# Gate/up projection by 2x2 block algebra: two weight sums made by accumulating DMAs, 18 of 22 tiles by it in place of 14

## The chip, the cores and the metric

The kernel runs on one core of a Trainium2 chip. The metric is the device time of one execution in microseconds. The kernel before took 859.75 us (median of 3 runs, 854.94 to 861.74).

## The reference

One layer of a hybrid decoder for 512 tokens of width 1024, in float32: an RMS norm, an input projection, two causal mixers (HGRN2 and gated DeltaNet), their gated merge, an output projection and a residual, and then a SwiGLU feed-forward block. The change lies in the feed-forward block:

```python
v = rms_norm(h, pre_ffn_w)
gate, up = jnp.split(jnp.einsum('btd,df->btf', v, w_gate_up), 2, axis=-1)
f = jnp.einsum('btf,fd->btd', jax.nn.silu(gate) * up, w_down)
return h + rms_norm(f, post_ffn_w)
```

Here v is 512 x 1024, w_gate_up is 1024 x 5632 (2816 gate and 2816 up columns) and w_down is 2816 x 1024.

## The kernel before, in words

**Numbers.** Each float32 operand of a product is split in two: `hi`, a rounded copy made on ScalarE (ACT), and `lo`, the rest, made by a subtraction on VectorE (DVE). A product is then three matmuls on TensorE (PE): hi x hi, hi x lo, lo x hi (L116 to L118, or L1010 to L1012).

**Stages.** Input projection and mixers, merge, `out_proj` (from about 430 to 490 us), `ffn` (gate and up products and SiLU, L1022, to 713 us) and `down` (L1102, to the end). The feed-forward width 2816 is cut in 22 tiles of 128 columns, `ft` 0 to 21 in the loop of L1076. A tile has a gate weight block g and an up weight block u, each 128 partitions x 1024 values: the first 512 are the rows of w_gate_up that belong to the first half of v's width, the other 512 those of the second half.

**Direct tiles** (before: ft 0, 1, 4, 7, 10, 13, 16, 19). `wload` (L99) loads g and then u into a `raw` buffer (512 KB each, two buffers of that tag), splits it into `whi` and `wlo` (three buffers of each), and 8 x 3 matmuls of 512 columns follow for each. Then ACT and DVE work out silu(gate) * up.

**Tiles by block algebra** (the others; `winograd`, L959, Winograd's variant of Strassen). The 2x2 matrix of weights is B11 = first half of g, B12 = first half of u, B21 and B22 = second halves of g and u. The 2x2 matrix of activations is v cut in token halves and width halves; its sums S1 to S4 are made once by `block_sums` (L924). Seven products of half the width and half the tokens replace eight: 7 x 4 x 3 matmuls of 256 columns. Four sums of weight blocks are needed in every tile. They are made on DVE: `t13`, one instruction over 1024 values that makes two of them, and `t24`, two instructions of 512 values. `t13` and `t24` lie in the two `raw` buffers. Seven operands (three blocks and four sums) are split by `operand` (L913), two to one `whi`/`wlo` buffer. The blocks themselves come by four SP DMAs of 256 KB into `raw = slot(5 + ft % 2)`, so two tiles have such a slot. The products accumulate in three PSUM tiles X, Wb and Y; DVE combines them with five instructions (`s15`, `s16`, `c22`, `c12`, `c21`), ACT copies `s1`. Product 6, `c21` and the SiLU of a tile (`flush`, L1062) come after products 0 and 1 of the next tile.

**Order.** A scheduler that works at build time puts the instructions of each engine in an order by priority, and allots buffers in turn by tag; at run time each engine and each DMA queue takes its instructions strictly in that order and waits on semaphores. `winograd` makes its weight sums and splits under a raised priority, loads have a higher one. In `ffn` the SP queue issues all weight loads; the POOL (GpSimd) engine has no work in the tile loop and no instruction after 489 us.

Of the kernel before, what the change touches and what calls it, by code (L numbers as in the profile page):

```python
# [9 lines left out]
F32 = mybir.dt.float32  # L10
# [4 lines left out]
ALU = mybir.AluOpType  # L15

P = 128
# [6 lines left out]
NF = DFF // P  # L24
EPS = 1e-6
NEG = -30000.0
HG_LEVELS = (64, 32, 16, 8, 4, 2, 1)
HG_MASKS = (16, 8, 4, 2, 1)

# [14 lines left out]
class K:  # L44
# [570 lines left out]
    def hg_attn(self, c, out):  # L615
# [20 lines left out]
        yield  # L636
        for lev in HG_LEVELS[:-1]:
            v = lambda x: x.rearrange("p h (n two t) -> p (h n) two t", two=2, t=lev)
# [194 lines left out]
    def out_proj(self):  # L833
# [4 lines left out]
        for nh in range(2):  # L838
            for lst, tile_, nm in ((pmw, self.hct, "post_mix_w"), (pfw, self.st, "pre_ffn_w")):
                t = tile_()  # L840
                lst.append(t.rearrange("p h t -> p (h t)"))
                nc.gpsimd.dma_start(out=lst[nh], in_=self.I[nm][nh * 512:nh * 512 + 512].partition_broadcast(P))
        W = []
        for i in range(8):
# [9 lines left out]
            for j in range(2):  # L854
                raw = self.dct((P, 512))
                nc.sync.dma_start(out=raw, in_=self.I["w_out"][i, :, j * 512:j * 512 + 512])
                self.split(h_[:, j, :], l_[:, j, :], raw, nc.gpsimd if i % 2 else None)
            W.append((h_, l_))
        self.h = []
# [64 lines left out]
    def block_sums(self, A, tmp, dst):  # L924


        hi, lo = A
        H, L = slice(256, 512), slice(0, 256)
        g = self.nc.gpsimd
        out = dict(A11=(0, L), A12=(1, L), A22=(1, H))  # L930
        out = {n: [[x[i][:, k, t] for k in range(4)] for x in A] for n, (i, t) in out.items()}
        S_ = [([], []) for _ in range(4)]
        for j in (slice(0, 2), slice(2, 4)):
            def block(i, t, eng=None):
                a = tmp()
                self.tt(a, hi[i][:, j, t].bitcast(F32), lo[i][:, j, t].bitcast(F32), ALU.add, eng)
                return a

            def put(i, src):
                d = dst(i, j)  # L940
                self.split(d[0], d[1], src)
                for o, x in zip(S_[i], d):
                    o += [x[:, 0], x[:, 1]]

            a21, a22 = block(0, H), block(1, H)
            self.tt(a22, a21, a22, ALU.add)
            put(0, a22)
            a11 = block(0, L, g)
            self.tt(a21, a11, a21, ALU.subtract)
            put(2, a21)  # L950
            self.tt(a22, a22, a11, ALU.subtract)
            put(1, a22)
            a12 = block(1, L, g)
            self.tt(a12, a12, a22, ALU.subtract)
            put(3, a12)
        out.update({f"S{i + 1}": S_[i] for i in range(4)})
        return out

    def winograd(self, raw, A, c12, c21, c22):  # L959

        nc = self.nc
        with self.tc.high_priority(offset=200):
            B11, _, B22, B21 = (raw[:, i] for i in range(4))
            t13, t24 = (self.wp.tile([P, 1040], F32, tag="raw", name=self.name("raw"), bufs=2)[:, :1024]
                        .rearrange("p (i n) -> p i n", i=2) for _ in range(2))
            self.tt(t13, raw[:, 1:3], raw[:, 0:2], ALU.subtract)
            self.tt(t24[:, 0], B22, t13[:, 0], ALU.subtract)
            self.tt(t24[:, 1], B21, t24[:, 0], ALU.subtract)  # L970
            W = [[t.rearrange("p (k f) -> p k f", k=4) for t in self.operand(x)]
                 for x in (B11, t13[:, 0], t24[:, 0], B21, t13[:, 1], B22, t24[:, 1])]
        X, Wb, Y = (f((P, 256)) for f in (self.mm_ps, self.dps, self.hps))
        prod = lambda i, a, ps, start: self.product(i, W[i], A[a], ps, start)
        s1, s15, s16 = (self.ftmp() for _ in range(3))
        now = self.tc.high_priority

        def first():
            prod(0, "A11", X, True)
            with now():  # L980
                nc.scalar.copy(s1, X)
            prod(1, "S1", Wb, True)
            with now():
                self.tt(s15, Wb, s1, ALU.add)

        def second():
            prod(2, "S2", Y, True)
            with now():
                self.tt(s16, Y, s1, ALU.add)
            prod(3, "A12", X, False)  # L990
            prod(4, "S3", Y, False)
            with now():
                self.tt(c22, Y, s15, ALU.add)
            prod(5, "S4", Wb, False)
            with now():
                self.tt(c12, Wb, s16, ALU.add)

        def third():
            prod(6, "A22", Y, False)
            with now():  # L1000
                self.tt(c21, Y, s1, ALU.add)

        return X, first, second, third

    def product(self, i, W, A, ps, start):
        wh, wl = W
        ah, al = A
# [14 lines left out]
    def ffn(self):  # L1022

        nc = self.nc
        A = nc.scalar
        self.half = self.fhalf = None
        gt = []

        def gslot(i):
            if i % 4 == 0:  # L1030
                gt.append(self.slot((4, 13, 11, 12, 14, 15)[i // 4], [P, 4, S]))
            return gt[i // 4][:, i % 4, :]

        def mms(ps, w, ts):
            for k in range(KD):
                self.mm3(ps[:, ts], w[0][:, k, :], w[1][:, k, :], self.vhi[k // 4][:, k % 4, ts],
                         self.vlo[k // 4][:, k % 4, ts], k == 0, k == KD - 1)

        load = lambda ft, gu: self.wload(self.I["w_gu"][ft, gu], (P, KD, P))

        def evac(t, g, u):
            with self.tc.high_priority():
                self.sigmoid(t, g)
                self.tt(t, t, g, ALU.mult)
                self.tt(t, t, u, ALU.mult)

        bank = lambda gu: self.hps((P, 512)) if gu else self.mm_ps()

        first = [(0, 0), (0, 1), (1, 0)]
        ws = {p: load(*p) for p in first}  # L1050
        pss = {p: bank(p[1]) for p in first}
        for half in range(2):
            for p in first:
                mms(pss[p], ws[p], slice(half * 256, half * 256 + 256))
        sp = [self.slot(i, [P, 4, 2, 256]) for i in (14, 15)]
        sp = iter([t[:, i] for t in sp for i in range(4)])
        so = [self.slot(i, [P, 2, 4, 256], F32R) for i in range(4)]
        L = self.block_sums((self.vhi, self.vlo), lambda: next(sp), lambda i, j: (so[i][:, 0, j], so[i][:, 1, j]))
        lo, hi = slice(0, 256), slice(256, 512)
        pending = None  # L1060

        def flush():  # L1062
            nonlocal pending
            if pending:
                X, third, g, u, t = pending
                third()
                A.activation(t[:, lo], X, AF.Exp, scale=-1.0)
                A.activation(t[:, hi], g[:, hi], AF.Exp, scale=-1.0)
                A.activation(t, t, AF.Ln, bias=self.one)
                A.activation(t, t, AF.Exp, scale=-1.0)  # L1070
                self.tt(t[:, lo], t[:, lo], X, ALU.mult)
                self.tt(t[:, hi], t[:, hi], g[:, hi], ALU.mult)
                self.tt(t, t, u, ALU.mult)
            pending = None

        for ft in range(NF):  # L1076
            if ft < 2 or ft % 3 == 1:
                for gu in range(2):
                    if (ft, gu) not in ws:
                        pss[ft, gu] = bank(gu)  # L1080
                        mms(pss[ft, gu], load(ft, gu), slice(0, S))
                    if gu == 0:
                        flush()
                evac(gslot(ft), pss[ft, 0], pss[ft, 1])
                continue
            with self.tc.high_priority():
                raw = self.slot(5 + ft % 2, [P, 4, 512])

                for gu in range(2):
                    src = self.I["w_gu"][ft, gu].rearrange("p (a b) -> p a b", a=2)  # L1090
                    nc.sync.dma_start(out=raw[:, gu], in_=src[:, 0])
                    nc.sync.dma_start(out=raw[:, 3 - gu], in_=src[:, 1])
            g, u = self.hct((P, 512)), self.hct((P, 512))
            X, p1, p2, p3 = self.winograd(raw, L, u[:, lo], g[:, hi], u[:, hi])
            p1()
            flush()
            p2()
            pending = X, p3, g, u, gslot(ft)
        flush()
        self.gt = gt  # L1100
# [116 lines left out]
def layouts(i):  # L1217
# [28 lines left out]
    t = np.arange(P)  # L1246
    cm = [np.eye(P), t[:, None] <= t[None, :], np.where(t[:, None] <= t[None, :], 0.0, NEG)]
    blk = lambda h: ((t[:, None] // (2 * h) == t[None, :] // (2 * h))
# [22 lines left out]
```

## Time and profile before

| | |
|---|---|
| median of 3 runs | 859.75 us (854.94 to 861.74) |
| the profiled execution | 856.85 us, span 855.1 us |
| PE busy | 823.5 us (96%) |
| DVE busy | 581.2 us (68%) |
| ACT busy | 487.2 us (57%) |
| POOL busy | 137.4 us (16%) |
| DMA | 96.43 MB, mean 113 GB/s |
| granted clock of PE | 0.984 of full speed over the span, 1.00 from 400 to 800 us |

A busy time is the time in which an engine executes at least one instruction, and the durations of neighbouring instructions overlap: what an engine needs for one is the distance between the starts of two that follow each other without a wait. The matmuls above all are pipelined. A group of instructions is written as line, engine, operation, out<-in with the program's tile names, and shape; tiles that come from `slot` appear as `s`.

### The profile page before, as it was taken

To read this page: it belongs to the slowest core of one execution; us is meant where nothing else is said; L and a number is where in the kernel's file an instruction comes from. 1 tells how busy PE (TensorE), PEld (TensorE's weight loads), DVE (VectorE), ACT (ScalarE), POOL (GpSimd) and SP (SyncE) were. 2 spreads that over 40 slices of the span, in tenths; PEclk is the share of its full clock that TensorE was granted. 3 is DMA by queue.
4 is the path that set the end of the run, shared out by engine and by line. 5 is a ranking of instruction groups with operands and counts; after the bars stand their busy time and mean duration, and the time that the engine had idled before them with its cause. 6 is when DMAs were issued, how large, how long until landed. Compare 5 with 4: busy or idle time off the path is not lost.

```text
span 855.1 us, 12329 instructions
## 1 busy us (share of the span) xinstructions
PE 823.5 (96%) x4684; PEld 695.8 (81%) x4684; DVE 581.2 (68%) x903; ACT 487.2 (57%) x888; POOL 137.4 (16%) x182
## 2 busy tenths in 40 slices
PE   8998999999999998999999999999999999999995
PEld 8986887788877777888888898999999998876774
DVE  4598779518478788622574697787787787557545
ACT  6648788755475666755443464545555456445443
POOL 1320168300054545300010300000000000000000
PEclk9999999959999999999999999999999999999999
DMA  8425432501051123522211313232322405556552
GB/s 295 152 75 196 125 101 95 155 26 50 26 185 50 50 75 99 170 91 88 96 62 50 124 41 109 91 107 99 122 76 100 148 5 168 174 173 212 182 170 101
DMA packets 34315, 96.43 MB, mean 113 GB/s; under 512 B 4112, under 2 KB 4528, under 8 KB 34128
## 3 DMA queue, kind: packets, MB, share of 16 engines
q1 hardware_dynamic: 32112, 88.65, 31.5%
q0 software_dynamic: 2144, 6.99, 3.1%
q8 instruction: 37, 0.61, 0.3%
q14 instruction: 22, 0.18, 0.1%
HBM read 90.90 MB, written 4.73 MB: 112 GB/s over the span
## 4 chain that ended last, share of the span: by engine, by line
PE 56%; DMA 11%; DVE 9%; POOL 4%; ACT 4%; issue 3%; DVEq 0%; ACTq 0%; SPq 0%; POOLq 0%
DMA raw<-in_w_down_dram 8%; PE mm L117 7%; PE mm L118 7%; PE mm L116 7%; POOL s L147 4%; DVE wlo L109 4%; ACT whi L108 3%; DVE hct L147 2%; PE hps L1011 2%; PE hps L1010 2%; PE hps L1012 2%; PE mm L869 2%; PE mm L868 2%; PE mm L867 2%; PE hps L118 2%
## 5 line engine op out<-in xcount | busy, mean ns | idle before, releaser
L109 DVE TENSOR_TENSOR wlo<-raw,whi 128x1024 fp32r<-128x1024 f32 x108 | 135.7, 1257 | 121.3 <-ACT whi L108 120.2
L116 PE MATMUL mm<-s,whi 128*128 128x512 f32 (+1 forms) x496 | 195.3, 394 | 0.0
L117 PE MATMUL mm<-s,whi 128*128 128x512 f32 (+1 forms) x496 | 195.0, 393 | 0.0
L118 PE MATMUL mm<-s,wlo 128*128 128x512 f32 (+1 forms) x496 | 194.6, 392 | 0.1
L108 ACT CAST whi<-raw 128x1024 fp32r<-128x1024 f32 x108 | 113.0, 1046 | 92.3 <-PE mm L117 39.1
L118 PEld LDWEIGHTS mm<-s,wlo 128*128 128x128 f32 x496 | 94.0, 190 | 19.8 <-DVE wlo L109 0.6
L116 PEld LDWEIGHTS mm<-s,whi 128*128 128x128 f32 x496 | 94.2, 190 | 19.3 <-issue 0.2
L117 PEld LDWEIGHTS mm<-s,whi 128*128 128x128 f32 x496 | 94.1, 190 | 18.7
L147 POOL TENSOR_TENSOR s<-s,dct 128x512 f32<-128x512 f32 (+1 forms) x9 | 12.7, 1435 | 391.6 <-DVE s L150 360.6
L121 ACT CAST whi<-raw 128x512 fp32r<-128x512 f32 (+1 forms) x64 | 38.9, 617 | 30.2 <-PE mm L1011 10.1
L121 ACT CAST whi<-s 128x512 fp32r<-128x512 f32 x42 | 25.9, 617 | 47.1 <-PE mm L117 21.4
L1010 PE MATMUL hps<-s,whi 128*128 128x256 f32 x168 | 47.2, 281 | 0.4 <-DVE hct L147 0.4
L1011 PE MATMUL hps<-s,whi 128*128 128x256 f32 x168 | 47.2, 281 | 0.1
L1012 PE MATMUL hps<-s,wlo 128*128 128x256 f32 x168 | 46.9, 279 | 0.0
L147 POOL TENSOR_TENSOR hct<-s 128x256 f32<-128x256 f32 (+1 forms) x55 | 43.4, 818 | 21.3 <-DVE hct L147 8.3
L147 DVE TENSOR_TENSOR wlo<-raw,whi 128x512 fp32r<-128x512 f32 (+1 forms) x64 | 43.5, 688 | 3.9 <-ACT whi L121 3.0
L147 DVE TENSOR_TENSOR hct<-hct,s 128x256 f32<-128x256 f32 (+1 forms) x63 | 32.7, 559 | 2.0 <-ACT hct L609 1.0
L147 POOL TENSOR_TENSOR s<-s 128x126 f32<-128x126 f32 (+22 forms) x62 | 32.3, 521 | 9.7 <-DMA s<-scr 4.9
L1010 PEld LDWEIGHTS hps<-s,whi 128*128 128x128 f32 x168 | 31.5, 188 | 0.9 <-DVE hct L147 0.6
L1011 PEld LDWEIGHTS hps<-s,whi 128*128 128x128 f32 x168 | 31.6, 188 | 0.6 <-DVE s L147 0.3
L1012 PEld LDWEIGHTS hps<-s,wlo 128*128 128x128 f32 x168 | 31.7, 189 | 0.0
L1011 PE MATMUL mm<-s,whi 128*128 128x256 f32 x112 | 31.5, 281 | 0.0
(329 smaller groups left out, 1943.2 us busy)
## 6 DMA issues: line engine op xcount, KB each, us to landing
raw<-in_w_in_a_dram SPq DMA_DIRECT2D x44, 512.0 KB, 3.4
raw<-in_w_down_dram SPq DMA_DIRECT2D x44, 512.0 KB, 3.4
s<-in_w_gu_dram SPq DMA_DIRECT2D x56, 256.0 KB, 4.0
raw<-in_w_gu_dram SPq DMA_DIRECT2D x16, 512.0 KB, 3.5
raw<-in_w_o_dram SPq DMA_DIRECT2D x8, 512.0 KB, 3.4
dct<-in_w_out_dram SPq DMA_DIRECT2D x16, 256.0 KB, 3.4
raw<-in_w_iab_dram SPq DMA_DIRECT2D x8, 260.0 KB, 5.9
s<-in_xT_dram SPq DMA_DIRECT2D x8, 256.0 KB, 6.0
```

Of the source, the lines that this page charges most:

```text
L108: nc.scalar.copy(hi[:, :n], raw[:, :n])
L109: nc.vector.tensor_tensor(out=lo[:, :n], in0=raw[:, :n], in1=hi[:, :n].bitcast(F32), op=ALU.subtract)
L116: mm(ps, lh, rh, start=start, stop=False)
L117: mm(ps, lh, rl, start=False, stop=False)
L118: return mm(ps, ll, rh, start=False, stop=stop)
L121: self.nc.scalar.copy(hi, src)
L147: (eng or self.nc.vector).tensor_tensor(out=out, in0=a, in1=b, op=op)
L867: T.matmul(ps, mh, wh, start=k == 0, stop=False)
L868: T.matmul(ps, mh, wl, start=False, stop=False)
L1010: mm(ps, wh[:, k, :], ah[k], start=start and k == 0, stop=False, skip_group_check=True)
L1011: mm(ps, wh[:, k, :], al[k], start=False, stop=False, skip_group_check=True)
L1012: mm(ps, wl[:, k, :], ah[k], start=False, stop=k == 3, skip_group_check=True)
```

## The change

Two of the four weight sums are no longer made by DVE. One SP DMA loads (B11, B12) into a buffer of their own, and a DMA issued from POOL's queue then adds (B12, B22) to it while it transfers, which gives B11 + B12 and B12 + B22. Signs of the other sums, of the activation sums S1 to S4 and of the combinations follow. DVE keeps two additions of 512 values in a tile, both in place. The buffers of these sums take turns: of three tiles in a row, two have one of the two `raw` buffers (one load and one accumulating DMA of 512 KB) and the third has two buffers of the `st` tag (two loads and two accumulating DMAs of 256 KB). B11, B21 and B22 are loaded as before, in one DMA of 512 KB and one of 256 KB. The direct tiles are now 0, 1, 8 and 15, so 18 tiles go by block algebra, six in a row three times.

```diff
--- before.py
+++ after.py
@@ -24,6 +24,7 @@
 NF = DFF // P
 EPS = 1e-6
 NEG = -30000.0
+DIRECT = (0, 1, 8, 15)
 HG_LEVELS = (64, 32, 16, 8, 4, 2, 1)
 HG_MASKS = (16, 8, 4, 2, 1)
 
@@ -943,7 +944,7 @@
                     o += [x[:, 0], x[:, 1]]
 
             a21, a22 = block(0, H), block(1, H)
-            self.tt(a22, a21, a22, ALU.add)
+            self.tt(a22, a21, a22, ALU.subtract)
             put(0, a22)
             a11 = block(0, L, g)
             self.tt(a21, a11, a21, ALU.subtract)
@@ -951,25 +952,22 @@
             self.tt(a22, a22, a11, ALU.subtract)
             put(1, a22)
             a12 = block(1, L, g)
-            self.tt(a12, a12, a22, ALU.subtract)
+            self.tt(a12, a12, a22, ALU.add)
             put(3, a12)
         out.update({f"S{i + 1}": S_[i] for i in range(4)})
         return out
 
-    def winograd(self, raw, A, c12, c21, c22):
+    def winograd(self, raw, u13, A, c12, c21, c22):
 
 
 
         nc = self.nc
         with self.tc.high_priority(offset=200):
-            B11, _, B22, B21 = (raw[:, i] for i in range(4))
-            t13, t24 = (self.wp.tile([P, 1040], F32, tag="raw", name=self.name("raw"), bufs=2)[:, :1024]
-                        .rearrange("p (i n) -> p i n", i=2) for _ in range(2))
-            self.tt(t13, raw[:, 1:3], raw[:, 0:2], ALU.subtract)
-            self.tt(t24[:, 0], B22, t13[:, 0], ALU.subtract)
-            self.tt(t24[:, 1], B21, t24[:, 0], ALU.subtract)
-            W = [[t.rearrange("p (k f) -> p k f", k=4) for t in self.operand(x)]
-                 for x in (B11, t13[:, 0], t24[:, 0], B21, t13[:, 1], B22, t24[:, 1])]
+            B11, B21, B22, U2 = (raw[:, i] for i in range(4))
+            self.tt(U2, B22, u13[0], ALU.add)
+            W = [self.operand(x) for x in (B11, u13[0], U2, B21, u13[1], B22)]
+            self.tt(B21, B21, U2, ALU.add)
+            W = [[t.rearrange("p (k f) -> p k f", k=4) for t in w] for w in W + [self.operand(B21)]]
         X, Wb, Y = (f((P, 256)) for f in (self.mm_ps, self.dps, self.hps))
         prod = lambda i, a, ps, start: self.product(i, W[i], A[a], ps, start)
         s1, s15, s16 = (self.ftmp() for _ in range(3))
@@ -981,7 +979,7 @@
                 nc.scalar.copy(s1, X)
             prod(1, "S1", Wb, True)
             with now():
-                self.tt(s15, Wb, s1, ALU.add)
+                self.tt(s15, Wb, s1, ALU.subtract)
 
         def second():
             prod(2, "S2", Y, True)
@@ -990,10 +988,10 @@
             prod(3, "A12", X, False)
             prod(4, "S3", Y, False)
             with now():
-                self.tt(c22, Y, s15, ALU.add)
+                self.tt(c22, s15, Y, ALU.subtract)
             prod(5, "S4", Wb, False)
             with now():
-                self.tt(c12, Wb, s16, ALU.add)
+                self.tt(c12, Wb, s16, ALU.subtract)
 
         def third():
             prod(6, "A22", Y, False)
@@ -1073,8 +1071,9 @@
                 self.tt(t, t, u, ALU.mult)
             pending = None
 
+        n = 0
         for ft in range(NF):
-            if ft < 2 or ft % 3 == 1:
+            if ft in DIRECT:
                 for gu in range(2):
                     if (ft, gu) not in ws:
                         pss[ft, gu] = bank(gu)
@@ -1085,13 +1084,24 @@
                 continue
             with self.tc.high_priority():
                 raw = self.slot(5 + ft % 2, [P, 4, 512])
-
-                for gu in range(2):
-                    src = self.I["w_gu"][ft, gu].rearrange("p (a b) -> p a b", a=2)
-                    nc.sync.dma_start(out=raw[:, gu], in_=src[:, 0])
-                    nc.sync.dma_start(out=raw[:, 3 - gu], in_=src[:, 1])
+                g, u = (self.I["w_gu"][ft, gu].rearrange("p (a b) -> p a b", a=2) for gu in range(2))
+
+                if n % 3 == 2:
+                    u13 = [self.st().rearrange("p h t -> p (h t)") for _ in range(2)]
+                    for i in range(2):
+                        nc.sync.dma_start(out=u13[i], in_=(g, u)[i][:, 0])
+                        nc.gpsimd.dma_start(out=u13[i], in_=u[:, i], accum_op=ALU.add)
+                else:
+                    t = self.wp.tile([P, 1040], F32, tag="raw", name=self.name("raw"), bufs=2)[:, :1024]
+                    t = t.rearrange("p (i n) -> p i n", i=2)
+                    nc.sync.dma_start(out=t, in_=self.I["w_gu"][ft, :, :, :512].rearrange("g p n -> p g n"))
+                    nc.gpsimd.dma_start(out=t, in_=u, accum_op=ALU.add)
+                    u13 = t[:, 0], t[:, 1]
+                n += 1
+                nc.sync.dma_start(out=raw[:, :2], in_=g)
+                nc.sync.dma_start(out=raw[:, 2], in_=u[:, 1])
             g, u = self.hct((P, 512)), self.hct((P, 512))
-            X, p1, p2, p3 = self.winograd(raw, L, u[:, lo], g[:, hi], u[:, hi])
+            X, p1, p2, p3 = self.winograd(raw, u13, L, u[:, lo], g[:, hi], u[:, hi])
             p1()
             flush()
             p2()
```

## Rows read from the trace of the kernel before

**Rows 1.** Windows: busy time by engine, clock, DMA share, GB/s; steady tiles, then the seam.

```profile
core 0: us, PE busy (x) PEld busy (x) DVE busy (x) ACT busy (x) POOL busy (x), PEclk, DMA share, GB/s
573.00:604.00 31.00, 31.00 (x219) 28.93 (x219) 24.29 (x41) 16.06 (x30) 0.00 (x0) 1.00 0.29 102
714.00:718.00 4.00, 2.47 (x11) 2.06 (x12) 3.22 (x8) 3.81 (x9) 0.00 (x0) 1.00 0.57 164
```

**Rows 2.** Timeline of PE: start, duration, instruction; a half direct tile, two products, a stall.

```profile
501.33 0.39 PE L116 MATMUL hps<-s,whi 128*128 128x512 f32 x1
...
506.88 0.28 PE L1010 MATMUL mm<-s,whi 128*128 128x256 f32 x1
...
509.73 0.28 PE L1010 MATMUL hps<-s,whi 128*128 128x256 f32 x1
...
514.92 0.28 PE L1012 MATMUL mm<-s,wlo 128*128 128x256 f32 x1
515.60 0.39 PE L1010 MATMUL hps<-s,whi 128*128 128x256 f32 x1 [0.40 <-DVE hct L147]
```

**Rows 3.** Timeline of SP: first load of a tile, three periods of the pattern.

```profile
572.22 0.33 SPq L1091 DMA_DIRECT2D s<-in_w_gu_dram  x1
...
603.14 0.33 SPq L1091 DMA_DIRECT2D s<-in_w_gu_dram  x1
...
664.90 0.33 SPq L1091 DMA_DIRECT2D s<-in_w_gu_dram  x1
```

**Rows 4.** Waits, 480 to 720 us: who for whom, us in total, times, longest.

```profile
ACT whi L121 <- PE mm L117: 21.9, 7, 4.3
DVE hct L147 <- PE dps L1012: 10.4, 13, 1.1
DVE raw L147 <- DMA s<-in_w_gu_dram: 3.1, 4, 1.7
```

**Rows 5.** Timeline of DVE around the first tiles by block algebra.

```profile
487.31 1.41 DVE L150 SCALAR_TENSOR_TENSOR hct<-dct,sm,st 128x512 f32<-128x512 f32 x2 [1.07 <-ACT sm L830]
...
497.99 1.21 DVE L109 TENSOR_TENSOR wlo<-raw,whi 128x1024 fp32r<-128x1024 f32 x1
...
508.29 0.69 DVE L147 TENSOR_TENSOR wlo<-s,whi 128x512 fp32r<-128x512 f32 x1
508.89 1.22 DVE L147 TENSOR_TENSOR raw<-s 128x1024 f32<-128x1024 f32 x1
510.03 0.41 DVE L147 TENSOR_TENSOR hct<-dps,hct 128x256 f32<-128x256 f32 x1
```

**Rows 6.** DMA issues: out<-in, queue, count, KB each, us from issue to landing.

```profile
s<-in_w_gu_dram SPq DMA_DIRECT2D x56, 256.0 KB, 4.0
raw<-in_w_gu_dram SPq DMA_DIRECT2D x16, 512.0 KB, 3.5
...
scr<-dct POOLq DMA_DIRECT2D x1, 1024.0 KB, 9.3
...
st<-in_post_ffn_w_dram POOLq DMA_DIRECT2D x2, 256.0 KB, 3.9
```

**Rows 7.** Timeline of POOL, its last instructions.

```profile
478.73 6.02 POOL L147 TENSOR_TENSOR s<-s,s 128x512 f32<-128x512 f32 x4 [46.29 <-PE mm L868]
488.36 0.55 POOL L1131 DMA_DIRECT2D st<-in_post_ffn_w_dram  x1 [3.62 <-DVE hct L150]
```

**Rows 8.** Timeline of PE at the seam from the last tile to the down projection.

```profile
713.30 0.28 PE L1012 MATMUL hps<-s,wlo 128*128 128x256 f32 x1
715.53 0.50 PE L1121 MATMUL dps<-whi,hct 128*128 128x512 f32 x1 [1.95 <-ACT hct L121]
```

**Rows 9.** Timeline of ACT at the seam.

```profile
711.78 1.05 ACT L108 CAST whi<-raw 128x1024 fp32r<-128x1024 f32 x1 [1.42 <-DMA raw<-in_w_down_dram]
714.13 1.04 ACT L108 CAST whi<-raw 128x1024 fp32r<-128x1024 f32 x1 [1.30 <-DVE wlo L109]
715.08 1.63 ACT L121 CAST hct<-s 128x256 fp32r<-128x256 f32 x5
```

## The prediction

> **What bounds the kernel now.** I read the table of busy times first, then windows over the feed-forward block, then the timelines there. The changed code runs from about 480 to 713 us. In a steady stretch of 31 us PE is busy all the time at granted clock 1.00 (the upper level, 2.4 GHz), DVE 24.3, ACT 16.1 us, the DMA engines 0.29 of it [rows 1]. So the reader is to see that a tile costs what its matmuls cost. The timeline gives that price: the up half of a direct tile starts at 501.33 and the next tile at 506.88, 5.55 us for 24 matmuls of 512 columns; two products of the block algebra, 24 matmuls of 256 columns, last from 506.88 to 509.73, 1.425 us each [rows 2]. The loads confirm it: three periods of two tiles by block algebra and one direct tile take 664.90 - 572.22 = 92.68 us, 30.89 each [rows 3], as PE's own work is 2 x 9.98 + 11.10 = 31.06. The waits say how far ahead the splits run: ACT stands idle for PE to give back weight buffers, 21.9 us in the costliest of several such groups [rows 4]. Splits are thus early by about the six operands that three weight buffers hold.
>
> **The change part by part.**
>
> *PE.* Four tiles change kind. A direct tile costs 2 x 5.55 = 11.10 us, the other kind 7 x 1.425 = 9.98; by the period it is (30.89 - 11.10) / 2 = 9.90. The difference is 1.12 or 1.20, for four tiles 4.5 to 4.8. I take **-4.6 us**, all on the path as long as PE stays the bound.
>
> *DVE.* The removed instruction over 1024 values costs 508.89 to 510.03, 1.14 us; the two additions that stay are of the kind with a pitch of 0.60 (508.29 to 508.89) [rows 5]. A direct tile has two subtractions of 1024 and two multiplications of 512 values: 2 x 1.14 + 2 x 0.60 = 3.5. From 24.3 us in a period a tile by block algebra takes (24.3 - 3.5) / 2 = 10.4, and 9.3 after the change, beside 9.9 of PE. In the runs of six there is no direct tile in which DVE catches up, so it goes from 78% to about 93%. Its instructions that combine products come late before PE does, since it now waits for PE there (10.4 us in one group [rows 4]), and that wait is slack. I take nothing, and keep 0 to 0.1 us for each of 18 tiles, 2 us, as the upper end.
>
> *SP.* Three or four issues for a tile in place of four, 0.33 us for the first [rows 3]; SP is idle between. Nothing. The order matters more: a load of the sums' buffer stands on SP ahead of the same tile's plain loads, and waits for its buffer. In a run of six that buffer was freed by the tile three places earlier, the slot by the tile two places earlier, so nothing is held up.
>
> *POOL and the accumulating DMAs.* 24 issues at 0.55 us on an engine with no work there after 489 us [rows 7]. Only the first may stand near the 6.02 us of activation sums at 478.73 [rows 7]; its load can go long before, so nothing, or up to 1 us where it holds them up. How long an accumulating DMA takes, no row shows. On the same queue a plain load of half its size landed after 3.9 us, a store of twice its size after 9.3 [rows 6]; I take 6.0 and keep both ends. From the freed buffer to a finished sum it is then 3.5 (load) + 0.55 + 6.0 = 10 us, 8 to 13.4 by the ends. Room in a run of six: three tiles, 29.7 us, less about 6 us by which splits lead, 24 us. **Hidden there.**
>
> Two places have less room. After the direct tiles 8 and 15 the buffer was held by that tile's gate weights. By the order of weight buffers these are split about 2 us before the direct tile's first matmul, and the first product with a sum comes 11.1 + 1.4 + 1.4 us later (a deferred product of the tile before lies between): 16 us of room against 10 and about 2 for the sum and its split. At the lower end of the price nothing is lost, at 13.4 it is about even; what is queued behind the waiting DVE addition (combinations of the tile before) may cost PE up to 2 us. I take **+0.3 each, +0.6**.
>
> The other place is tile 3. Its buffer comes free when the second up tile is split, 497.99 + 1.21 = 499.2 [rows 5]; the sum is finished at 499.2 + 10 = 509.3, by the ends 507.2 to 512.6. Before, its first sum ran at 508.89. If the addition stands there, DVE is held for 0 to 3.7 us with activation sums behind it, for which PE already waits now (514.92 to 515.60, about 0.55 us more than a pitch [rows 2]). Against this DVE has 1.14 us less to do ahead. Bounds -1.1 and +3.7; at 6.0 it is +0.4 - 0.9, so **-0.5**.
>
> *DMA engines.* A tile moved 1.05 MB, and a period of 3.15 MB keeps the engines busy for 0.29 x 31 = 9.0 us [rows 1], 2.86 us a MB. After the change a tile moves 1.31 MB plainly and 0.52 MB accumulating. Were these as fast, it is 5.2 of 9.9 us; they become the bound where an accumulated byte costs over 4.1 times a plain one: (1.31 + 0.52 x 4.1) x 2.86 = 9.9. Hence no cost, with a rival behind it. The Trainium skill (Collectives: The Full Stack, "The bandwidth ceiling: the fold count and why AG ≠ RS ≠ AR") says that a reducing transfer runs at half a copy's rate, for its two reads and not for the addition; by that factor of two, an estimate, a tile keeps the DMA engines busy for 6.7 us, and the sum stays. No row here shows one.
>
> *The seam to the down projection.* PE is idle there from 713.42 to 715.53 [rows 8], behind ACT, which waits 1.42 us for a load and 1.30 for a buffer before it turns to the activations [rows 9]. Tile 21 would now have its sums elsewhere, so both load buffers come free a tile earlier. That can give back 0 to 2.1 us. But the first down weights wait for weight buffers as now, and the third load for the first one's split; I take 0 and keep -2.1.
>
> Signs are free. The sum: -4.6 + 0.6 - 0.5 = **-4.5 us**, 856.85 - 4.5 = 852.4 for an execution like the profiled one. That one lies 2.9 under the median of 859.75, so on the scale of the median **855.2 us**.
>
> **The rivals.**
>
> A. *Accumulating is so slow that the DMA engines bound the tile.* Place: every tile in the runs of six. It decides from a factor of 4.1 on. At five it is (1.31 + 0.52 x 5) x 2.86 = 11.2 us, 1.3 over PE for 18 tiles: 859.75 - 4.5 + 23 = 878 us, slower. For it: the large store on POOL's queue moved 1 MB in 9.3 us, where SP's loads take 3.5 for half of that [rows 6]. Against: that is a factor of 1.3, far from 4.1. Chance 0.12.
>
> B. *The gain is spent on waits of DVE.* The sums come late at tiles 3, 9 and 16, at the upper ends 3.7 + 2 x 2, and DVE at 93% delays a product now and then: the 4.6 us are given back, about 860 us (857 to 863). For it: DVE takes its order strictly, and it is the fullest engine after PE. Against: the waits of ACT and DVE for PE [rows 4]. Chance 0.22.
>
> C. *DVE's relief and the freed buffers remove the old stalls too.* 4.6 + 1.1 + 2.1 = 7.8: 852 us. For it: both stalls are real [rows 2, 8]. Against: the load chain behind the seam. Chance 0.15.
>
> D. *POOL can't write its descriptors while DVE is busy.* With DVE idle for some 0.6 us of a tile, an issue may wait a tile's length. In the runs of six the room of 24 us takes it; at tiles 3, 9 and 16 sums would be some 5 us late each: 859.75 - 4.5 + 12 to 15, 868 us. Against: the issue at 488.36 took 0.55 us [rows 7] though DVE was on its two-input instructions until 488.72 [rows 5]. The Trainium skill (SBUF — State Buffer, its warning on "The 'DVE blocks DMA' trap (SWDGE)") states such a rule for DVE's two-port modes; the trace has no such delay at that issue. Chance 0.06.
>
> **How the numbers follow.** My forecast has 0.45. Its own range is 851 to 858, from the bounds at tile 3, the seam and the spread of the three runs. To hold eight in ten the range reaches to C below and B above: 850 to 864; what is left out is A, D and a little of B and C. About 1% (8.6 us) is what a measurement of this kernel tells from no change: under 851.2 lie the better half of C (0.09) and a tail of the forecast (0.05), faster 0.14; over 868.3 lie A, most of D and a tail of B, slower 0.18; within 0.68.
>
> **What would show it.** Right: in a run of six, PE busy all the time with first matmuls of neighbouring tiles 9.9 us apart, DVE near 9 us of that, POOL with issues of about 0.55 us, accumulating DMAs landing after 4 to 9 us, and no PE wait behind a DVE instruction that waits for one. Wrong: tiles longer than 10.2 us with the DMA share near 1 (A); PE gaps behind DVE at tiles 3, 9, 16 (B); the gaps near 515 and 714 gone (C); POOL issues of several us (D). Should the first accumulating DMA land only after 15 us or more, even the room in the runs of six is gone and the prediction fails altogether.

## The result, and the profile after

The changed kernel takes 866.3 us (median; 862.9 to 872.3) against 858.9 for the kernel before beside it: a ratio of 1.0098, 95% interval 1.0074 to 1.0122. It is slower by 7.4 us. The forecast was 855.2 us in a range of 850 to 864, so the time lies outside the range and on the other side of no change. The profiled execution took 864.88 us, 8.0 more than that of before. One trace below, that of e1, is of an execution longer than the rest of its kernel (874.3 us against 861.2 to 866.1), so places are read from it and not lengths.

The head of its page: span, busy times with their share and instructions, and TensorE's granted clock in 40 slices.

```profile
span 863.1 us, 12784 instructions
PE 824.6 (96%) x4828; PEld 702.0 (81%) x4828; DVE 578.9 (67%) x941; ACT 496.7 (58%) x916; POOL 157.9 (18%) x206
...
PEclk9999999969999999999999999999999999999998
```

These totals hide the result: PE's busy time rose by little, and the slow stretches are a few us long. I therefore cut each trace at two instructions, the first matmul of the block algebra and the first of the down projection. The table has the length of the stage between them (the feed-forward tiles), that from there to the end of the span, and the places where PE stood longer than a matmul's pitch, all of one profiled execution each.

| kernel | feed-forward, us | down, us | PE stands in the feed-forward, us |
|---|---|---|---|
| before | 208.6 | 139.6 | tile 3: 0.25 + 0.56; seam 2.1 |
| before, profiled again | 208.8 | 138.0 | the same places |
| after | 214.6 | 142.7 | tile 3: 1.63; 0.62; 0.59; tile 9: 2.44; tile 16: 3.42; seam 1.77 |
| after, profiled again | 211.7 | 142.6 | tile 3: 1.63; tile 9: 2.37; tile 16: 3.03; seam 1.69 |

From before to after the feed-forward tiles are 6.0 us longer and the down projection 3.1; what lies ahead is 1.1 shorter, 8.0 in all. Eighteen tiles of 9.9 us, two direct ones of 11.1 and a seam of 2.1 would be 202.5 us: the gain was there to be had, and 12.1 us were lost on top of it (9.2 in the second profile, which has neither the two small stands nor, as shown below, the low clock behind tile 9).

**A run of six** answers to [rows 1]. Windows of after (busy us and instructions of each engine, granted clock, share of the DMA engines, GB/s):

```profile
core 0: us, PE busy (x) PEld busy (x) DVE busy (x) ACT busy (x) POOL busy (x), PEclk, DMA share, GB/s
592.00:616.00 24.00, 24.00 (x206) 24.00 (x206) 20.56 (x40) 13.85 (x27) 2.56 (x3) 1.00 0.73 172
```

PE is busy all the time at clock 1.00, DVE 86% of it, the DMA engines 0.73 (0.68 to 0.75 in other stretches and in the second profile). The three POOL instructions are accumulating issues, 0.85 us each. Their price is in the list of DMA issues (KB each, median us to landing):

```profile
raw<-in_w_gu_dram POOLq DMA_DIRECT2D x12, 512.0 KB, 6.7
...
st<-in_w_gu_dram POOLq DMA_DIRECT2D x12, 256.0 KB, 5.1
```

**Tile 9, behind the direct tile 8**, is where it goes wrong. First DVE (start, duration, instruction, and in brackets the idle time before it and what ended that):

```profile
564.07 1.23 DVE L110 TENSOR_TENSOR wlo<-raw,whi 128x1024 fp32r<-128x1024 f32 x1 [0.26 <-ACT whi L109]
...
568.23 0.42 DVE L148 TENSOR_TENSOR hct<-dps,hct 128x256 f32<-128x256 f32 x1
576.93 0.69 DVE L148 TENSOR_TENSOR s<-s,raw 128x512 f32<-128x512 f32 x1 [8.29 <-DMA raw<-in_w_gu_dram]
577.54 0.68 DVE L148 TENSOR_TENSOR wlo<-s,whi 128x512 fp32r<-128x512 f32 x1
...
585.71 0.42 DVE L148 TENSOR_TENSOR hct<-dps,hct 128x256 f32<-128x256 f32 x1
586.04 1.28 DVE L148 TENSOR_TENSOR wlo<-s,whi 128x512 fp32r<-128x512 f32 x2
587.24 0.41 DVE L148 TENSOR_TENSOR hct<-hps,hct 128x256 f32<-128x256 f32 x1
```

The split at 564.07 frees the buffer. POOL issued the accumulation at 571.27, once the load had landed:

```profile
571.27 0.85 POOL L1098 DMA_DIRECT2D raw<-in_w_gu_dram  x1 [7.59 <-DMA raw<-in_w_gu_dram]
```

The instruction at 576.93 is the new addition, `U2 = B22 + sum`, the only one of the tile's preparations that DVE does before it splits anything. It is first in DVE's order behind 568.23 and waits 8.29 us for its sum. DVE takes its order strictly, so what stands behind it waits too. Not all of the 8.29 us held up work that was ready, as ACT's order shows:

```profile
572.62 0.62 ACT L122 CAST whi<-s 128x512 fp32r<-128x512 f32 x1 [5.83 <-PE mm L118]
...
576.93 0.62 ACT L122 CAST whi<-raw 128x512 fp32r<-128x512 f32 x1 [3.19 <-DMA raw<-in_w_gu_dram]
```

The tile's first split, at 577.54 on DVE, needs the rounded copy that ACT makes at 572.62, once PE has given back a weight buffer. So it could have run from about 573.2, some four us earlier. The sum itself is the second operand, so ACT's own order stands still for it too, for 3.19 us, with the SiLU of two tiles behind. The same addition stands at tile 16 for 9.28 us (ACT 4.23) and at tile 3 for 2.22. Now PE, in the same columns, the first and last matmul of the direct tile and the matmul that stalls:

```profile
567.09 0.40 PE L117 MATMUL mm<-s,whi 128*128 128x512 f32 x1
...
579.39 0.40 PE L119 MATMUL hps<-s,wlo 128*128 128x512 f32 x1
...
585.15 0.28 PE L1010 MATMUL mm<-s,wlo 128*128 128x256 f32 x1
587.71 0.39 PE L1008 MATMUL hps<-s,whi 128*128 128x256 f32 x1 [2.28 <-DVE hct L148]
588.39 0.41 PE L1009 MATMUL hps<-s,whi 128*128 128x256 f32 x1
```

During the 8.3 us PE never stops: it has the direct tile's matmuls and weights that were split earlier. The stall comes eight us after the sum has landed (it begins at about 585.3), when PE has used up the lead and needs a bank that DVE's combination at 587.24 clears. From the landing at 576.9 to that combination DVE has 10.3 us of work in its queue and almost no idle time. In this execution the stall also has a tail. Windows of after behind it, and behind the one at tile 16:

```profile
587.00:588.00 1.00, 0.29 (x2) 0.29 (x3) 1.00 (x3) 0.00 (x0) 0.00 (x0) 1.00 0.98 377
588.00:589.00 1.00, 1.00 (x7) 1.00 (x7) 0.85 (x2) 0.00 (x0) 0.00 (x0) 0.57 0.68 168
589.00:590.00 1.00, 1.00 (x7) 1.00 (x6) 0.00 (x0) 0.00 (x0) 0.77 (x1) 0.50 0.98 342
590.00:591.00 1.00, 1.00 (x7) 1.00 (x6) 0.42 (x1) 0.00 (x0) 0.09 (x1) 0.50 1.42 322
591.00:592.00 1.00, 1.00 (x8) 1.00 (x8) 0.00 (x0) 0.00 (x0) 0.00 (x0) 0.72 0.70 98
...
660.00:668.00 8.00, 4.74 (x27) 4.74 (x28) 4.82 (x10) 1.53 (x4) 0.85 (x1) 0.79 0.67 190
```

The granted clock falls to 0.50, its lower level of 1.2 GHz, for some 3.3 us, and the pitch of a matmul goes from 0.119 to 0.214 us. Fifteen matmuls from 588.17 take 3.21 us in place of 1.79, and with the slower ones at both ends 1.6 us are lost once PE had work again. (Nothing is read from the one DMA share above 1.) Tile 9 thus costs 2.44 + 1.62 = 4.06 us (22 pitches from 585.15 take 6.68 us in place of 2.62), tile 16 by the same count 3.42 + 1.61 = 5.03. The tail does not always come. In the second profile PE stood 2.37 us at tile 9, and the clock behind that stayed at 1.00 (window of after2):

```profile
588.39:592.39 4.00, 4.00 (x34) 4.00 (x34) 1.57 (x3) 0.98 (x2) 0.85 (x1) 1.00 0.85 233
```

**The down projection** runs its loads, casts and matmuls in the same order as before, but ACT waits longer for loads. Waits from 718 us to the end (total us, times, longest), of before and of after:

```profile
ACT whi L108 <- DMA raw<-in_w_down_dram: 33.5, 29, 2.7
```

```profile
ACT whi L109 <- DMA raw<-in_w_down_dram: 42.1, 31, 2.9
```

### The profile page after: what moved, and what is told of

Its sections match the earlier page's. It is cut to its first block, busy times and chain, and to the rows that moved or that the text cites. A ratio compares the mean times of both kernels' runs of the same rounds, so it can differ in the third digit from the quotient of the medians.

```text
span 863.1 us, 12784 instructions
## 1 busy us (share of the span) xinstructions
PE 824.6 (96%) x4828; PEld 702.0 (81%) x4828; DVE 578.9 (67%) x941; ACT 496.7 (58%) x916; POOL 157.9 (18%) x206
## 4 chain that ended last, share of the span: by engine, by line
PE 47%; DMA 16%; DVE 13%; ACT 5%; POOL 4%; issue 3%; DVEq 0%; SPq 0%; ACTq 0%; POOLq 0%
DMA raw<-in_w_down_dram 9%; PE mm L118 6%; PE mm L117 6%; PE mm L119 6%; DVE wlo L110 4%; POOL s L148 4%; DVE s L148 4%; DMA raw<-in_w_gu_dram 3%; ACT whi L109 3%; PE hps L1008 2%; DVE hct L148 2%; PE hps L1009 2%; PE hps L1010 2%; PE mm L870 2%; PE mm L869 2%
## 5 line engine op out<-in xcount | busy, mean ns | idle before, releaser
L117 PE MATMUL mm<-s,whi 128*128 128x512 f32 (+1 forms) x464 | 182.7, 394 | 0.0
L118 PE MATMUL mm<-s,whi 128*128 128x512 f32 (+1 forms) x464 | 182.3, 393 | 0.0
L119 PE MATMUL mm<-s,wlo 128*128 128x512 f32 (+1 forms) x464 | 181.9, 392 | 0.0
L109 ACT CAST whi<-raw 128x1024 fp32r<-128x1024 f32 x100 | 104.6, 1046 | 82.8 <-DMA raw<-in_w_down_dram 42.1
L117 PEld LDWEIGHTS mm<-s,whi 128*128 128x128 f32 x464 | 88.1, 190 | 18.2 <-ACT sm L344 0.2
L118 PEld LDWEIGHTS mm<-s,whi 128*128 128x128 f32 x464 | 88.0, 190 | 17.5
L122 ACT CAST whi<-s 128x512 fp32r<-128x512 f32 x90 | 53.4, 618 | 58.5 <-PE hps L1009 24.1
L1008 PE MATMUL hps<-s,whi 128*128 128x256 f32 x216 | 62.1, 287 | 6.5 <-DVE hct L148 6.4
L1009 PE MATMUL hps<-s,whi 128*128 128x256 f32 x216 | 61.6, 285 | 1.4 <-DVE s L148 1.4
L1010 PE MATMUL hps<-s,wlo 128*128 128x256 f32 x216 | 61.3, 284 | 0.0
L148 DVE TENSOR_TENSOR wlo<-s,whi 128x512 fp32r<-128x512 f32 x90 | 59.7, 684 | 1.1
L1008 PEld LDWEIGHTS hps<-s,whi 128*128 128x128 f32 x216 | 41.4, 192 | 7.5 <-DVE hct L148 6.6
L1009 PEld LDWEIGHTS hps<-s,whi 128*128 128x128 f32 x216 | 41.7, 193 | 1.7 <-DVE s L148 1.6
L1008 PE MATMUL dps<-s,whi 128*128 128x256 f32 x144 | 40.9, 284 | 0.0
L1009 PE MATMUL dps<-s,whi 128*128 128x256 f32 x144 | 40.8, 283 | 0.0
L1010 PE MATMUL dps<-s,wlo 128*128 128x256 f32 x144 | 40.6, 282 | 0.0
```

The costliest lines, as they stand in the source:

```text
L109: nc.scalar.copy(hi[:, :n], raw[:, :n])
L117: mm(ps, lh, rh, start=start, stop=False)
L118: mm(ps, lh, rl, start=False, stop=False)
L119: return mm(ps, ll, rh, start=False, stop=stop)
L122: self.nc.scalar.copy(hi, src)
L148: (eng or self.nc.vector).tensor_tensor(out=out, in0=a, in1=b, op=op)
```

## The experiments

The theory: the new addition waits for a late sum at the head of DVE's queue; PE pays when its lead is gone, and at some of the stands again through the clock. The first rival: runs of six tiles leave DVE or the DMA engines no room whatever the order. The second: accumulating itself is what costs. Ratios are to the kernel before, run beside each.

**e1, the buffers' turn moved by one.** The sum tile right behind each direct tile takes the buffer that no direct tile uses.

```diff
-                if n % 3 == 2:
+                if n % 3 == 0:
```

> The turn of the buffers is shifted by one: the tiles whose number among the block-algebra tiles divides by 3 (tiles 2, 5, 9, 12, 16, 19) have the two st buffers, so the first tile after each direct tile no longer waits for the buffer that held the direct tile's gate weights, and the second up tile's buffer serves tile 4 instead of tile 3. Theory 1 (late sums: DVE stands 8.3 us at tile 9 and as long at tile 16, PE then 2.4 and 3.4 us with the clock at 0.5 for some 3 us after, and 1.6 us at tile 3): these gaps go, 866.3 - 10 = 856 us, DVE's longest wait for a weight sum under 3 us. Rival 2 (runs of six tiles load DVE and the DMA engines too much whatever the buffer): no change, 865 to 867.

1.0091 [1.0066, 1.0117]: nothing gained, against what the theory said. The wait did not go, it moved to the second tile behind the direct one, which now shares the buffer. A second kind of wait is there as well, for the plain load of `B22` (waits of DVE, columns as above):

```profile
532.06 0.69 DVE L148 TENSOR_TENSOR s<-s,st 128x512 f32<-128x512 f32 x1 [3.53 <-DMA s<-in_w_gu_dram]
...
584.48 0.69 DVE L148 TENSOR_TENSOR s<-s,raw 128x512 f32<-128x512 f32 x1 [8.37 <-DMA raw<-in_w_gu_dram]
...
662.95 0.69 DVE L148 TENSOR_TENSOR s<-s,raw 128x512 f32<-128x512 f32 x1 [8.53 <-DMA raw<-in_w_gu_dram]
```

So it is not the neighbour's place that decides, but that a direct tile and a sum share a buffer at all. PE's longest stand in this trace, from 533 to 537 us, follows the addition at 532.06, which stands far from any direct tile of the loop and waits for no sum.

**e2, no accumulating DMA.** Both are removed, so that the additions of the up weights into the sums are left out; loads, splits and products stay.

> The changed kernel without the accumulating DMAs: the additions of the second weight block are left out, the loads into the same buffers stay. Theory 1 (late sums): DVE waits for the plain load alone, 6 us earlier; the gaps at tiles 9 and 16 go, 855 to 857 us. Rival 2, in the form that DVE is overloaded in runs of six: DVE's work is the same, so 863 to 867; in the form that DMA traffic is too much: a share of 0.45 in place of 0.6 to 0.7 and some 860.

0.997 [0.995, 0.999]; feed-forward 202.4 us, where the sum above has 202.5, with no PE stand but the seam. All that was lost there hangs on the accumulations. This alone does not say whether by their traffic or by their lateness.

**e6, the same DMAs overwriting in place of accumulating** (`accum_op` dropped; the up weights replace the sum). The bytes, the order and the waits stay.

> The changed kernel with the second DMA on POOL's queue plain in place of accumulating: the addition is left out (it overwrites). Prices the accumulation alone. If it costs two reads: the 512 KB DMA lands after 4 us in place of 6.7, the waits at tiles 9 and 16 shrink by that to 5 to 6 us and the kernel takes 859 to 863 us. If the price is POOL's queue: it lands after 6 to 7 us and the time stays at 865 to 867.

1.0000 [0.9972, 1.0027]. A plain transfer of the same bytes on the same queue:

```profile
raw<-in_w_gu_dram POOLq DMA_DIRECT2D x12, 512.0 KB, 4.7
st<-in_w_gu_dram POOLq DMA_DIRECT2D x12, 256.0 KB, 3.3
```

Accumulating thus costs 2.0 and 1.8 us more until it lands. With that taken away DVE waits 5.93 and 6.67 us at tiles 9 and 16, and ahead of the seam PE stands once, 0.99 us at tile 16. Measured from the direct tile's first matmul, the data is there after 7.5 and 8.2 us in place of 9.8 and 10.8, and PE's stands shrink by about as much, from 2.44 to nothing and from 3.42 to 0.99. Data that comes about two and a half us earlier gives back some 8 us (1.0098 to 1.0000): what an addition waits first eats a lead that costs nothing, and only then PE's time.

**e3, 18 tiles with the sums made on DVE as before.** The kernel before with the new set of direct tiles.

```diff
-            if ft < 2 or ft % 3 == 1:
+            if ft in (0, 1, 8, 15):
```

> The kernel before with the direct tiles 0, 1, 8 and 15: 18 tiles by block algebra, all four sums on DVE. If DVE's need is the sum of busy times (10.4 us a tile against 9.9 of PE): DVE bounds the runs of six by 0.5 us a tile, 858.9 - 4.6 + 8 = 862 us. If it is the pitches (about 9.6 us): PE stays the bound, 854 to 857 us, and the accumulating DMAs weren't needed for 18 tiles.

1.0006 [0.9985, 1.0026]. Feed-forward 204.6, 4.0 less than before, at DVE 37.53 of 40 us in a run of six, with PE busy throughout (windows of e3, columns as above):

```profile
590.00:630.00 40.00, 40.00 (x339) 39.64 (x338) 37.53 (x70) 24.73 (x49) 0.00 (x0) 1.00 0.31 107
```

Runs of six don't overload DVE, even with the old sums on it: the first rival falls for DVE. For the DMA engines e5 and e10 below answer it. But the down projection takes 141.8 us, 2.2 and 3.8 more than in the two profiles of before, and no accumulating DMA is in this kernel.

**e4, the old 14 tiles with the accumulating sums.**

```diff
-            if ft in DIRECT:
+            if ft < 2 or ft % 3 == 1:
```

> The changed kernel's accumulating DMAs with the direct tiles of the kernel before (0, 1, 4, 7, 10, 13, 16, 19): 14 tiles by block algebra, runs of two. Theory 1: what costs is the direct tile in the loop, since the two load buffers it takes are those of the sums behind it; six of them are in the loop in place of two, so this is slower than the kernel before by 6 times 1 to 4 us (DVE has more time to catch up here), 865 to 880 us. Rival 2 (runs of six are the trouble): as the kernel before, 857 to 860.

1.0087 [1.0057, 1.0117]: as slow as the change, without any of the four new tiles. Each of the six direct tiles in the loop is now followed by a late sum; these are six of the nine waits (DVE's waits from 505 to 720 us):

```profile
DVE s L148 <- DMA raw<-in_w_gu_dram: 45.4, 9, 8.2
```

Feed-forward 217.8, down 136.9. Together with e3: the feed-forward loss goes with accumulations, the down projection's with the set of direct tiles.

**e8, the addition held back.** The only edit is an order: `U2` is issued behind the split of the tile's first operand.

```diff
-            self.tt(U2, B22, u13[0], ALU.add)
-            W = [self.operand(x) for x in (B11, u13[0], U2, B21, u13[1], B22)]
+            W = [self.operand(B11)]
+            with self.tc.issue_after(self.lasttt.ins):
+                self.tt(U2, B22, u13[0], ALU.add)
+            W += [self.operand(x) for x in (u13[0], U2, B21, u13[1], B22)]
```

> The changed kernel with one edge of order: DVE's addition of B22 to a sum (the first that reads an accumulating DMA's result) stands behind the split of the same tile's first operand. Buffers, loads and DMAs stay as they are. Theory 1a (the sums are late only because the build-time order puts this addition some 8 us before it is needed, so that DVE's whole queue waits there): DVE's waits at tiles 9 and 16 fall from 8.3 and 9.3 us to some 2, PE's gaps there and the low clock behind them go, 854 to 858 us where the kernel before has 858.9. Theory 1b (the buffers come free too late whatever the order): the wait moves, the gap stays, 863 to 867 us, as the shift of the buffers' turn had no effect.

1.0031 [1.0008, 1.0055], below the change's whole interval. The same DMAs land in the same buffers, and the addition waits 2.21 and 3.61 us where it waited 8.29 and 9.28:

```profile
573.04 0.69 DVE L148 TENSOR_TENSOR wlo<-s,whi 128x512 fp32r<-128x512 f32 x1 [4.63 <-ACT whi L122]
575.94 0.69 DVE L148 TENSOR_TENSOR s<-s,raw 128x512 f32<-128x512 f32 x1 [2.21 <-DMA raw<-in_w_gu_dram]
...
648.49 0.69 DVE L148 TENSOR_TENSOR s<-s,raw 128x512 f32<-128x512 f32 x1 [3.61 <-DMA raw<-in_w_gu_dram]
```

The addition's wait overstates what this does for DVE. Before it DVE now stands 4.63 and 4.58 us for the first split, so its idle time at the two places goes from 8.29 to 6.84 us and from 9.28 to 8.19. What moves is that split, now ahead of the sum, and the addition of the tile behind, which stood in the middle of tile 9's splits (579.37) and now comes after the combination that PE needs. PE's stands go from 2.44 to 0.69 us and from 3.42 to 2.06. Of these 1.75 and 1.36 us, 0.8 and 0.4 go with sums that landed that much earlier after the direct tile's first matmul; the order is worth the rest, 1.0 us at each place. The stand at tile 3, the two small ones and the low clock at tile 9 are gone too, and no addition waits over 1.5 us for `B22`'s plain load any more. The sums are late for the order that is left as well, in which ACT's cast of the sum still comes second; no run moves that cast.

**e5, direct tiles at the ends**, `DIRECT = (0, 1, 20, 21)`, with e1's turn: a run of 18 without a direct tile in it.

> The shifted turn (as in e1) with the direct tiles 0, 1, 20 and 21: one run of 18 tiles by block algebra with no direct tile inside. Theory 1: no place with a late sum inside the run, PE busy all the time: 853 to 857 us. Rival 2 (runs load DVE or the DMA engines too much): a run of 18 without a pause is slower than runs of six, over 866 us, with PE gaps all along.

0.9949 [0.9922, 0.9976], no PE stand over 0.5 us, and that at the seam gone. Three times the run's length costs nothing, so runs of tiles by block algebra were not the trouble. **e12** has the same `DIRECT` alone, without e1's turn or the hold.

> The changed kernel with direct tiles 0, 1, 20 and 21 and nothing else: neither the shifted turn of e5 nor the edge of e8. Theory 1: with no direct tile in the loop only the late sum at tile 3 is left (1.6 us), 0.994 to 0.997 of the kernel before. If the place of the direct tiles weren't the cause: 1.005 to 1.01 as the changed kernel.

0.9978 [0.9959, 0.9996]. Its runs spread from 851.8 to 863.5, and the profiled one is the 863.5: PE stands 1.63 us at tile 3, and then 3.80, 2.35 and 1.26 us behind additions that wait for a plain load. This is the first of them:

```profile
533.56 0.69 DVE L148 TENSOR_TENSOR s<-s,raw 128x512 f32<-128x512 f32 x1 [4.28 <-DMA s<-in_w_gu_dram]
```

So the early addition is a risk with a plain load as well as with a sum. That it bites in some runs and not in others is what the spread suggests; one trace can't show it.

**e10, the hold and the direct tiles at the ends.**

> The edge of order of e8 with the direct tiles 0, 1, 20 and 21 and the buffers' turn of the changed kernel. With no direct tile in the loop the buffers are never late, so the edge adds nothing but safety: as e5, 0.994 to 0.997 of the kernel before. If the edge itself costs (DVE later with the first sum in each tile): above e5 by more than 2 us.

0.9931 [0.9901, 0.9961], 850.7 us: the best version, 0.7% below the kernel before. Feed-forward 200.5, the ideal being 18 x 9.9 + 2 x 11.1 = 200.4. Windows of e10:

```profile
530.00:590.00 60.00, 60.00 (x512) 60.00 (x511) 52.37 (x104) 37.80 (x74) 7.46 (x9) 1.00 0.73 186
```

PE is busy throughout at DMA share 0.73, though the large accumulations land after 7.5 us, later than in the changed kernel. No addition waits over 1.5 us here: a transfer may take longer where its buffer comes free early enough. Against e12 the intervals just touch, and e5's overlaps, so what the hold adds to the ends is likely but not settled. **e9** drops the last two direct tiles as well, `DIRECT = (0, 1)` with the hold.

> The edge of order of e8 with 20 tiles by block algebra and the direct tiles 0 and 1 alone. Against e10 two tiles more at 1.1 to 1.2 us each: PE saves 2.3 us, 0.990 to 0.993 of the kernel before, if the last tile's sums and splits leave the seam to the down projection as it is (2 us of PE gap come back with a block-algebra tile at the end: then no gain over e10, 0.993 to 0.996).

0.9956 [0.9937, 0.9974]: feed-forward 199.8, and the seam is back with 1.73 us. No gain over e10.

The kernels before and after were profiled once more for the table above.

> The kernel before, unchanged, for a second profile. From the first down-projection matmul to the end it took 139.6 us in the first profile, 141.8 to 142.7 in the kernels with direct tiles 8 and 15, 140.6 in those with 20 and 21. If executions differ by that much, 139 to 143 here; if the order of the tiles sets it, 139.6 again to 0.5. The feed-forward stage: 208.6 us again to 0.5.

> The changed kernel, unchanged, for a second profile. Theory 1: the same PE gaps at tiles 3, 9 and 16 with DVE's waits of 8 to 9 us, feed-forward stage 214.6 us to 1.5. Rival: gaps that come and go from one execution to the next. Down projection 142.7 to 0.5 if the tile set decides it.

The three large places repeat, with DVE waiting 8.24 and 7.98 us at tiles 9 and 16. The two small stands (0.62 and 0.59 us) do not; in the first profile they came after an addition that waited 2.34 us for a plain load.

## Why the prediction was wrong

*The step that failed* is the one on the two places after direct tiles, "+0.3 each, +0.6". They cost 4.1 and 5.0 us in the first profile. Its arithmetic of arrival nearly held at tile 9: the load went out 1.8 us before the direct tile's first matmul (2 said), and the sum was there 11.6 us later (10 said, 8 to 13.4), because the load took 5.4 us in place of 3.5. PE's first product with it came 15.7 us after the load went out (16 said), so that product never waited. What failed is the comparison with that product, and the "about 2 for the sum and its split" behind the arrival. From the landing to the combination that PE waited for, DVE had 10.3 us of queued work: splits and combinations, the SiLU of two tiles, and an addition for the tile behind. The addition stands in front of this queue for 8.3 and 9.3 us, and for about the last four of them work behind it was ready, and ACT's cast of the sum holds ACT's order for 3.2 and 4.2. "What is queued behind the waiting DVE addition" was named, with "combinations of the tile before" and at most 2 us; it was more than a tile's work of DVE (8.5 us by the window of the run of six). And no term had the clock's tail of 1.6 us, which came behind the stand at tile 16 in both profiles and behind that at tile 9 in one. e2 and e6 show that the late sums are the cause, and e10, where PE is full with the DMA engines as busy as here, that it is not the load on those engines. e8 shows that the place of the additions in the order is a part of it, about 1.0 us of PE's stand at each place; how the rest divides between DVE's and ACT's order was not tried.

*Also missing*: the down projection stood in the sum with nothing and takes 3.1 us more in these two profiles (3.0 to 4.7 over all four). e3 and e4 tie that to the set of direct tiles. What in the set does it, I can't say: the instructions stand in the same order, ACT waits 42.1 us for loads in place of 33.5, and with both ends direct (e10) the stage takes 140.7. The granted clock is not it: over the stage's first 70 us it is 1.00 in all four profiles, and behind that 0.96 to 0.97. How the loads and buffers stand when the stage begins may matter; this was not tried.

*Tile 3*: -0.5 said, about +0.8 measured (1.63 us of PE's standing against 0.81), within its bounds; the 0.9 in "+0.4 - 0.9" stands in no row, as the removed instruction is 1.14. Two small stands (0.62, 0.59) add 1.2. The *seam* gave 0.3, as good as nothing.

*Right*: PE's -4.6 (e3 gets 4.0 with the old sums, e2 and e10 come to the ideal within 0.1 us). DVE stays under PE: 93% said, 86% measured; its 10.4 us a tile was too high, since e3 with all four sums needs 37.53 of 40 us, 9.3 a tile. The price of an accumulation: 6.0 said, 6.7 and 5.1 measured. "Hidden there" in the runs of six, also when they are 18 long. The DMA engines: a share of 0.73, where the traffic without any surcharge was 5.2 of 9.9 us and with the factor of two of the Trainium skill (Collectives: The Full Stack, "The bandwidth ceiling: the fold count and why AG ≠ RS ≠ AR") 6.7 of 9.9, or 0.68. The trace is nearer to that factor. e6, which moves the same bytes plainly, has the 5.2 of 9.9 (window of e6):

```profile
589.40:613.40 24.00, 23.81 (x202) 23.61 (x201) 21.73 (x43) 15.89 (x32) 1.62 (x3) 1.00 0.53 182
```

The landing times against e6's plain ones are in a ratio of 1.4 and 1.5. POOL's issue took 0.85 us, not 0.55, which is 0.3 of the 11.6 us to the sum at tile 9.

*The rivals*: A (the DMA engines as the bound) is refuted by 0.73 with PE full. B had the right mechanism and all three places, and still priced the two that matter at 2 us each, so that its 857 to 863 was too low as well. C fell: both stalls stayed. D (descriptors held up by DVE) is refuted: the accumulating issues took 0.85 us each (two of the 24 took 0.88 and 1.13), with DVE 86% busy, so nothing of it is seen in this kernel's additions and splits. The rule behind D, that GpSimd can't write descriptors while DVE is in its two-port modes, is the Trainium skill's (SBUF — State Buffer, its warning on "The 'DVE blocks DMA' trap (SWDGE)"); no issue here shows it.

The gap closes by the terms: 8.5 at the two places, 3.1 down, 1.3 at tile 3, 1.2 for the small stands, -0.3 seam, -1.1 ahead of the stage make 12.7 us; the profiled execution is 12.5 over the 852.4 forecast for it.

## What to carry to other kernels

The price of a late transfer is not only how late its data is for the engine that multiplies it. Find the first instruction of each in-order queue that reads it, and count the work behind that instruction up to the next one that the bound engine waits for: here it was ten us. An instruction that takes no scarce buffer may be ordered well ahead of its need, as these additions were, so tie it behind the work it should not overtake; in this kernel that gave back part of the loss, and taking the lateness away all of it. And where a few tiles of another kind share buffers with a chain of two dependent transfers, put them at the ends of the loop.

## What the runs showed of the hardware

The granted clock fell to 0.50 behind PE stands of 2.44 us (tile 9) and 3.42 us (tile 16), and behind e8's of 2.06 (0.50 from 660 to 662). It stayed at 1.00 behind stands of 2.37 us (tile 9 in the second profile), 2.1 us (the seam of the kernel before) and 1.63 us (tile 3), so the length of a stand alone doesn't tell which it will be. Each fall in the changed kernel's first profile lasted some 3.3 us and cost 1.6, two thirds of the stand itself at tile 9.

An accumulating DMA of 512 KB from DRAM into SBUF landed after 6.7 us and one of 256 KB after 5.1, where plain ones on the same queue took 4.7 and 3.3; an accumulating issue kept POOL for 0.85 us and a plain one (e6) for 0.54. In e10 the accumulating ones took 7.5 and 6.2. The landing times are medians of twelve.
